# Passing 20 grains of memory from the mixer to the feed-forward, pacing side work behind weight splits, and loading the mixer's weights a unit ahead

## The chip, the cores and the metric

The kernel runs on one core of a Trainium2 chip as a single program. Its engines are TensorE (PE, matrix products), VectorE (DVE), ScalarE (ACT), GpSimd (POOL) and SyncE (SP, which here only issues DMAs). Each works through its own list of instructions strictly in order, waiting where an instruction needs something that another engine or a DMA has not delivered. The metric is the time of one execution on the device in microseconds, smaller being better. Three runs of the kernel before took 2114.45, 2119.53 and 2125.24 us.

## The reference

One transformer-like layer over 2048 tokens of width 1024, all float32:

```python
h = rms_norm(x, norm1); p = h @ w_in                    # 1024 -> 2576
lru_x, lru_g, q, k, v, g, z = split(p)
lru_o = rg_lru(conv4(lru_x), ...) * gelu(lru_g)          # linear recurrence over time
gla_o = rms_norm(gla_chunk_causal(q*s, k, v, log_sigmoid(z @ w_alpha + b)/16)) * silu(g)
x = x + concat([lru_o, gla_o]) @ w_out                   # 1024 -> 1024
h = rms_norm(x, norm2)
gate, up = split(h @ w_ffn_in)                           # 1024 -> 2 x 2816
x = x + (silu(gate) * up) @ w_ffn_out                    # 2816 -> 1024
return rms_norm(x, final_norm)
```

## The kernel before

**Precision.** Every large product is made of three matmuls (`mm3`, L224 to L226). An operand `a` is split into `hi`, a cast to PE's reduced float32R done by ACT (L234), and `lo = a - hi`, done by DVE (L235). PE computes hi*hi, hi*lo and lo*hi. So no matmul of a weight can start before ACT and then DVE have split it, and the split waits for the raw weight's DMA.

**Stages.** The mixer runs over four blocks of 512 tokens (b = 0 to 3, up to about 750 us of the trace). Then the feed-forward's gate and up products run over two blocks of 1024 tokens (about 750 to 1680 us), in a scheme with seven half-size products in place of eight (`Gate.gate_up`), for 22 column groups j each. Then comes the down product (`Down`, to the end), with the same scheme. In a mixer block the feature projections, the gates of the recurrence, the q product, four recurrence scans on DVE (`lru_scan`, L477), the state updates (PE L604, DVE L619), the outputs `lru_out` with their gelus (L634), and the output product of the previous block follow each other. Norm1 of the next block loads x (L240), squares it on ACT (L195, which writes its squares into a scratch piece of memory), takes an rsqrt on DVE and scales x (L279).

**Memory.** Nearly all of the on-chip memory is two regions, cut into grains of 128 words per partition: `A` (tile `arena`, float32, 144 grains: raw loads, activations, scratch) and `R` (tile `arena_r`, float32R, 260 grains: split operands). `Space.alloc` picks free grains when the program is written, and prefers grains that were freed long ago (`since`, with a cost for those freed within the last RECENT = 12 frees). Reusing a grain makes the new writer wait for the last reader of the old contents: an activation, a cast, or a DMA store.

**Weights.** `Feed` keeps two (mixer) or three (gate) split units ready. In the mixer a unit is loaded and split in the same step: `unit` calls `load`, then `split` twice, then frees the raw weight. In the gate stage `gu_makers(j)` fetches four raw pieces and makes seven operands of them (`a11`, `s1`, `s2`, ...; sums at L730, L735, L745, L757), a few units ahead.

**Side work.** Beside the gate products, `spread` deals out other work over the slots (j, r): normalising and transposing the second block's input (`normed`), its differences, and the preparation of the down product's weights (`w2_sums`: sums at L1036, L1040, L1043, a cast on ACT at L1009, a subtraction on DVE at L1016, and two stores to a DRAM tile `w2c` by POOL's queue). `load_acc` loads the down product's accumulators (from `x2d`, by POOL's queue), `split_act` splits its first activations (L1113, L1114).

**Order.** The program is written in Python in one order, and a list scheduler then sets each engine's list by priorities and its own estimates of when things are ready. `tc.issue_after(ins)` makes the scheduler put what is written inside the block behind the instruction `ins`; it adds no wait on the chip. The copies that empty a PSUM bank after a gate product are L907; PE cannot start the next use of that bank earlier.

Of the kernel before, what the change touches and what calls it, by code (L numbers as in the profile page):

```python
# [7 lines left out]
F32 = mybir.dt.float32  # L8
# [29 lines left out]
A_GRAINS = 144  # L38
R_GRAINS = 260
A_BORDER = 48  # L40
# [48 lines left out]
class Space:  # L89
# [6 lines left out]
    def __init__(self, ap, grains):  # L96
        self.ap = ap
        self.n = grains
        self.used = [False] * self.n
        self.since = [0] * self.n  # L100
        self.clock = 0

    def alloc(self, words, key):
        need = -(-words // GRAIN)
        best = None
        run = 0
        for i in range(self.n):
            run = 0 if self.used[i] else run + 1
            if run >= need:
                a = i - need + 1  # L110
                cost = max(0, max(self.since[a : i + 1]) - self.clock + self.RECENT) // self.STEP
                k = (*key(a, need, cost), a)
                if best is None or k < best:
                    best = k
        assert best is not None, f"no room for {words} words; {self.used.count(False) * GRAIN} free"
        a = best[-1]
        for g in range(a, a + need):
            self.used[g] = True
        return self.ap[:, a * GRAIN : a * GRAIN + words], a, need
# [40 lines left out]
def hybrid_layer_kernel(  # L160
# [25 lines left out]

    def bank():
        return pp.tile([P, T], F32, tag="mm", name="mm", bufs=8)
# [42 lines left out]
    def split(src, n, low=False):  # L231
        b = pair(n, low)
        hi, lo = b.r(n)
        nc.scalar.copy(hi, src)  # L234
        nc.vector.tensor_sub(lo, src, hi.bitcast(F32))  # L235
        return b

# [5 lines left out]
    def unit(src, n=D):  # L243
        raw = load(src, n)
# [77 lines left out]

    def block_units(b):
# [17 lines left out]
    feed = Feed([(lambda s=s, n=n: unit(s, n)) for s, n in all_units], 2)  # L341
# [422 lines left out]
    def gu_feed(groups):  # L764
# [12 lines left out]
        def step(i):  # L777
            fetch(i)
            return makers[i]()
# [481 lines left out]
    for b in range(NB):  # L1261
# [7 lines left out]
                  lambda: gate_fetch(0)])  # L1269
    A.aged = True  # L1270
# [3 lines left out]
    for bi, blk in enumerate(blocks):  # L1274
# [14 lines left out]
        else:  # L1289
            spread([w2_sums(range(3, NJ // 2))], [55], 2, NJ - 2)  # L1290
        sums = iter(())
        for js in groups:
# [4 lines left out]
            for r in range(7):  # L1297
                for j, g in zip(js, gens):
                    run(g, 1)
                    for f in side.get((j, r), ()):  # L1300
                        f()
                if js[0] == 0:
                    run(late, 2 if bi else 1)
                if final and nb:
                    run(ahead, 3 if r else 1)
                if final and not nb:
                    if r in (1, 2):
                        down.load_act(r - 1)
                        down.load_acc(r - 1)
                    if r == 3:  # L1310
                        run(down.split_act(0))
# [75 lines left out]
```

## Time and profile before

| what | value |
|---|---|
| runs, median of 3 | 2119.53 us (2114.45 to 2125.24) |
| profiled execution, its own time | 2122.03 us |
| span of that execution, first to last instruction | 2120.3 us |
| PE busy | 2024.7 us (95%) |
| DVE busy | 1343.9 us (63%) |
| ACT busy | 888.5 us (42%) |
| mean granted TensorE clock | 0.981 of 2.4 GHz |

Read it from PE: it is the only engine near its limit, so the time is PE's work, plus the time in which it waited, plus what it lost while its clock stood at half. The average shares of the other engines say little; what matters is which instruction of theirs PE waited for, and what that one had waited for.

### The profile page before, as it was taken

Reading aid. Unit: us, or ns where it says so; the run is one execution under the profiler, and the core shown is the slowest. Engines: PE = TensorE matmul, PEld = TensorE weight load, DVE = VectorE, ACT = ScalarE, POOL = GpSimd, SP = SyncE. Lnnn points to the kernel's source line nnn. Section 1 sums busy time; section 2 is a strip of 40 time slices with the busy share of each in tenths; the row PEclk is TensorE's granted clock in tenths of the full one; section 3 lists DMA queues with packets and bytes.
Section 4 is the critical chain, followed back from the end, with each engine's and each line's share of the span. In section 5 each row is a group of like instructions: output and inputs, shape, how many; then the busy total and the mean of one; then the engine's idle time right before and its main releaser. Section 6 shows DMA issues by size and latency. Waiting matters only on the chain. (4 is left out here: it accounts for less than half of the span.)

```text
span 2120.3 us, 26570 instructions
## 1 busy us (share of the span) xinstructions
PE 2024.7 (95%) x9520; PEld 1661.4 (78%) x9520; DVE 1343.9 (63%) x2390; ACT 888.5 (42%) x1523; POOL 180.0 (8%) x216
## 2 busy tenths in 40 slices
PE   7889999979999999999999999999999999999997
PEld 6778778868887888887787887787778788888876
DVE  6475556555646586557776777677666465665676
ACT  5645635543573453443443554444433221121331
POOL 0000000000000000000111001111110222222110
PEclk9989999989999999999999999999999999999999
DMA  5132245234525553467557457567554946745632
GB/s 181 61 107 82 90 131 178 96 109 134 171 65 169 173 197 107 159 218 219 194 168 229 141 169 240 175 198 224 196 181 143 382 160 219 236 149 172 234 127 80
DMA packets 211174, 353.21 MB, mean 167 GB/s; under 512 B 19409, under 2 KB 95458, under 8 KB 211042
## 3 DMA queue, kind: packets, MB, share of 16 engines
q1 hardware_dynamic: 196898, 304.32, 45.0%
q0 software_dynamic: 14144, 47.20, 5.9%
q8 instruction: 74, 1.21, 0.2%
q14 instruction: 58, 0.48, 0.1%
HBM read 244.49 MB, written 106.95 MB: 166 GB/s over the span
## 5 line engine op out<-in xcount | busy, mean ns | idle before, releaser
L224 PE MATMUL mm<-arena_r 128*128 128x512 f32 (+1 forms) x2848 | 1116.4, 393 | 60.0 <-ACT arena_r L234 33.4
L225 PE MATMUL mm<-arena_r 128*128 128x512 f32 (+1 forms) x2848 | 1108.7, 389 | 6.5 <-DVE arena_r L235 4.8
L226 PE MATMUL mm<-arena_r 128*128 128x512 f32 (+1 forms) x2848 | 1102.6, 389 | 8.4 <-DVE arena_r L235 8.3
L224 PEld LDWEIGHTS mm<-arena_r 128*128 128x128 f32 x2848 | 540.9, 190 | 192.4 <-ACT arena_r L234 37.8
L234 ACT CAST arena_r<-arena 128x512 fp32r<-128x512 f32 (+1 forms) x638 | 377.4, 610 | 647.0 <-PE mm L225 341.4
L226 PEld LDWEIGHTS mm<-arena_r 128*128 128x128 f32 x2848 | 541.1, 190 | 120.5 <-DVE arena_r L235 12.0
L225 PEld LDWEIGHTS mm<-arena_r 128*128 128x128 f32 x2848 | 542.4, 190 | 112.8 <-DVE arena_r L235 9.6
L235 DVE TENSOR_TENSOR arena_r<-arena,arena_r 128x512 fp32r<-128x512 f32 (+1 forms) x638 | 422.1, 677 | 289.2 <-ACT arena_r L234 251.8
L1147 DVE TENSOR_TENSOR arena<-arena,mm 128x512 f32<-128x512 f32 x288 | 197.3, 687 | 149.1 <-PE mm L226 149.1
L1113 ACT CAST arena_r<-arena_r 128x896 fp32r<-128x896 f32 (+1 forms) x88 | 80.2, 916 | 307.5 <-PE mm L225 209.0
L1018 POOL DMA_DIRECT2D w2c<-arena x148 | 79.8, 541 | 870.7 <-ACT arena L1009 792.4
L1114 POOL TENSOR_TENSOR arena_r<-arena_r 128x896 fp32r<-128x896 f32 x40 | 85.6, 2140 | 314.6 <-PE mm L226 123.4
L195 ACT ACTIVATE arena<-arena 128x512 bf16<-128x512 f32 (+1 forms) x80 | 57.0, 712 | 75.0 <-DVE arena L1147 22.7
L907 ACT COPY arena<-mm 128x512 f32<-128x512 f32 x132 | 76.6, 580 | 14.4 <-PE mm L226 14.3
L1009 ACT CAST arena<-arena 128x512 fp32r<-128x512 f32 x74 | 45.6, 620 | 60.0 <-DMA w2c<-arena 13.8
L930 DVE TENSOR_TENSOR arena<-mm,arena 128x512 f32<-128x512 f32 x44 | 30.3, 689 | 56.9 <-PE mm L226 56.9
L626 POOL COPY stc<-arena 128x256 f32<-128x256 f32 x4 | 4.3, 1068 | 644.6 <-DVE arena L619 457.9
L1114 DVE TENSOR_TENSOR arena_r<-arena_r 128x896 fp32r<-128x896 f32 (+1 forms) x48 | 49.0, 1020 | 13.7 <-ACT arena_r L1113 11.4
L1016 DVE TENSOR_TENSOR arena<-arena 128x512 fp32r<-128x512 f32 x74 | 49.8, 688 | 12.2 <-ACT arena L1009 11.6
L730 DVE TENSOR_TENSOR arena<-arena 128x512 f32<-128x512 f32 x44 | 30.2, 687 | 26.3 <-DMA arena<-in_wgu_dram 15.3
L933 DVE TENSOR_TENSOR arena<-mm,arena 128x512 f32<-128x512 f32 x44 | 30.3, 689 | 23.7 <-PE mm L226 23.6
L922 DVE TENSOR_TENSOR arena<-mm,arena 128x512 f32<-128x512 f32 x44 | 30.2, 687 | 23.1 <-PE mm L226 23.1
(132 smaller groups left out, 1067.2 us busy)
## 6 DMA issues: line engine op xcount, KB each, us to landing
arena<-in_wgu_dram SPq DMA_DIRECT2D x176, 256.0 KB, 3.9
ad<-arena SPq DMA_DIRECT2D x148, 256.0 KB, 3.0
w2c<-arena POOLq DMA_DIRECT2D x148, 256.0 KB, 3.8
arena_r<-w2c SPq DMA_DIRECT2D x148, 256.0 KB, 5.3
arena_r<-ad SPq DMA_DIRECT2D x80, 448.0 KB, 3.5
arena<-in_wf_dram SPq DMA_DIRECT2D x40, 512.0 KB, 3.5
arena<-in_wo_dram SPq DMA_DIRECT2D x32, 512.0 KB, 3.9
arena<-in_w_dram SPq DMA_DIRECT2D x44, 256.0 KB, 4.0
```

Of the source, the lines that this page charges most:

```text
L195: nc.scalar.activation(b.ap.bitcast(BF16), src, AF.Square, accum_out=dst)
L224: nc.tensor.matmul(ps, lhsT=sh, rhs=mh, start=first, stop=False, skip_group_check=again)
L225: nc.tensor.matmul(ps, lhsT=sh, rhs=ml, start=False, stop=False, skip_group_check=again)
L226: nc.tensor.matmul(ps, lhsT=sl, rhs=mh, start=False, stop=last, skip_group_check=again)
L234: nc.scalar.copy(hi, src)
L235: nc.vector.tensor_sub(lo, src, hi.bitcast(F32))
L907: nc.scalar.copy(b.f(), ps[:, :n])
L1016: nc.vector.tensor_sub(b.f().bitcast(F32R), b.f(), hi.f())
L1018: nc.gpsimd.dma_start(w2c[k][:, m, i * T : (i + 1) * T], part.f())
L1113: nc.scalar.copy(hi, v)
L1114: (nc.gpsimd if i == 1 else nc.vector).tensor_tensor(lo, v, hi.bitcast(F32), op=ALU.subtract)
L1147: nc.vector.tensor_add(c, c, ps)
```

## The change

20 of the 144 grains of `A` become a separate tile, `swing`. During the mixer it is float32R and belongs to `R` (280 grains, `A` 124); before the gate products it is given back (`shrink`) and allocated anew as float32 in `A` (144 and 260 as before). Grains that were never used now count as freed long ago. The mixer's feed becomes `Units`: the raw weight of the next unit is loaded (`fetch`) before the present one is split, so two raw weights are held. `paced` writes side work behind the instructions of the last gate weight's split (both the ACT cast and the DVE subtraction, kept in `b.ins`), and each gate weight's making behind the split before it. The loads of the first two accumulators move from the last column group to group NJ - 3, and the second block's 55 pieces of weight preparation end one group earlier.

```diff
--- before.py
+++ after.py
@@ -35,8 +35,10 @@
 NCOL = 49
 
 GRAIN = 128
-A_GRAINS = 144
+A_GRAINS = 124
 R_GRAINS = 260
+
+SWING = 20
 A_BORDER = 48
 R_BORDER = 204
 
@@ -94,18 +96,34 @@
     STEP = 3
 
     def __init__(self, ap, grains):
-        self.ap = ap
-        self.n = grains
-        self.used = [False] * self.n
-        self.since = [0] * self.n
+        self.parts = []
+        self.used = []
+        self.since = []
         self.clock = 0
+        self.extend(ap, grains)
+
+    @property
+    def n(self):
+        return len(self.used)
+
+    def extend(self, ap, grains):
+        self.parts.append((self.n, ap))
+        self.used += [False] * grains
+        self.since += [-self.RECENT] * grains
+
+    def shrink(self):
+
+        first, _ = self.parts.pop()
+        assert not any(self.used[first:])
+        del self.used[first:], self.since[first:]
 
     def alloc(self, words, key):
         need = -(-words // GRAIN)
+        starts = {first for first, _ in self.parts}
         best = None
         run = 0
         for i in range(self.n):
-            run = 0 if self.used[i] else run + 1
+            run = 0 if self.used[i] else 1 if i in starts else run + 1
             if run >= need:
                 a = i - need + 1
                 cost = max(0, max(self.since[a : i + 1]) - self.clock + self.RECENT) // self.STEP
@@ -116,7 +134,8 @@
         a = best[-1]
         for g in range(a, a + need):
             self.used[g] = True
-        return self.ap[:, a * GRAIN : a * GRAIN + words], a, need
+        first, ap = max((p for p in self.parts if p[0] <= a), key=lambda p: p[0])
+        return ap[:, (a - first) * GRAIN : (a - first) * GRAIN + words], a, need
 
     def free(self, b):
         self.clock += 1
@@ -184,6 +203,11 @@
     A = Arena(Space(cp.tile([P, A_GRAINS * GRAIN], F32, name="arena"), A_GRAINS), A_BORDER)
     R = Arena(Space(cp.tile([P, R_GRAINS * GRAIN], F32R, name="arena_r"), R_GRAINS), R_BORDER)
 
+    def swing(dtype):
+        return cp.tile([P, SWING * GRAIN], dtype, tag="swing", name="swing", bufs=1)
+
+    R.space.extend(swing(F32R), SWING)
+
     def bank():
         return pp.tile([P, T], F32, tag="mm", name="mm", bufs=8)
 
@@ -231,17 +255,24 @@
     def split(src, n, low=False):
         b = pair(n, low)
         hi, lo = b.r(n)
-        nc.scalar.copy(hi, src)
-        nc.vector.tensor_sub(lo, src, hi.bitcast(F32))
+        b.ins = [nc.scalar.copy(hi, src).ins, nc.vector.tensor_sub(lo, src, hi.bitcast(F32)).ins]
         return b
+
+    pace = []
+
+    def paced(f, *args):
+
+        with ExitStack() as st:
+            for ins in pace:
+                st.enter_context(tc.issue_after(ins))
+            return f(*args)
 
     def load(src, n, low=False, queue=nc.sync):
         b = A.alloc(n, low)
         queue.dma_start(b.f(n), src)
         return b
 
-    def unit(src, n=D):
-        raw = load(src, n)
+    def unit(raw, n):
         v = raw.f(2, n // 2)
         b = [split(v[:, i, :], n // 2) for i in range(2)]
         A.free(raw)
@@ -319,6 +350,25 @@
             b = self.ready.pop(0)
             self.fill()
             return b
+
+    class Units(Feed):
+
+
+        def __init__(self, units, ahead):
+            self.units = list(units)
+            self.raws = []
+            super().__init__([lambda n=n: self.make(n) for _, n in units], ahead)
+
+        def fetch(self):
+            if self.units:
+                self.raws.append(load(*self.units.pop(0)))
+
+        def make(self, n):
+            if not self.raws:
+                self.fetch()
+            raw = self.raws.pop(0)
+            self.fetch()
+            return unit(raw, n)
 
     def block_units(b):
         u = [(wkz[i], 544) for i in range(4)]
@@ -338,7 +388,7 @@
 
     all_units = [u for b in range(NB) for u in block_units(b)]
     all_units += [(wo[n, i], D) for n in range(2) for i in range(4)]
-    feed = Feed([(lambda s=s, n=n: unit(s, n)) for s, n in all_units], 2)
+    feed = Units(all_units, 2)
 
     wal_b, zta_b = A.alloc(256), A.alloc(T)
     nxt = Norm1(0, 2)
@@ -776,7 +826,9 @@
 
         def step(i):
             fetch(i)
-            return makers[i]()
+            b = paced(makers[i])
+            pace[:] = b.ins
+            return b
 
         return Feed([lambda i=i: step(i) for i in range(len(makers))], 3), fetch
 
@@ -1267,6 +1319,8 @@
                   lambda: first.load_x(2)])
     prev.half(1, [lambda: run(first.combine(1)), lambda: first.load_x(3), lambda: run(first.combine(2)),
                   lambda: gate_fetch(0)])
+    R.space.shrink()
+    A.space.extend(swing(F32), SWING)
     A.aged = True
     late = first.combine(3)
     run(late, 1)
@@ -1287,7 +1341,9 @@
             spread([nb.differences(c) for c in range(4)], [6] * 4, 8, 12)
             spread([w2_sums(range(3))], [23], 12, NJ - 2)
         else:
-            spread([w2_sums(range(3, NJ // 2))], [55], 2, NJ - 2)
+            spread([w2_sums(range(3, NJ // 2))], [55], 2, NJ - 3)
+            for i in range(2):
+                side.setdefault((NJ - 3, 3 * i + 1), []).append(lambda i=i: down.load_acc(i))
         sums = iter(())
         for js in groups:
             gens = [blk.gate_up(j) for j in js]
@@ -1298,17 +1354,16 @@
                 for j, g in zip(js, gens):
                     run(g, 1)
                     for f in side.get((j, r), ()):
-                        f()
+                        paced(f)
                 if js[0] == 0:
-                    run(late, 2 if bi else 1)
+                    paced(run, late, 2 if bi else 1)
                 if final and nb:
-                    run(ahead, 3 if r else 1)
+                    paced(run, ahead, 3 if r else 1)
                 if final and not nb:
                     if r in (1, 2):
                         down.load_act(r - 1)
-                        down.load_acc(r - 1)
                     if r == 3:
-                        run(down.split_act(0))
+                        paced(run, down.split_act(0))
                     if r:
                         run(ahead, 2)
                 run(sums, 1)
```

The changed program has as many instructions on each engine as before; what differs is their order and where their data lie. Three places follow. The kernel's lines have moved: L195, L234/L235, L477, L575, L591, L634 of before are L219, L258, L527, L625, L641, L684 after; in the gate stage L730, L745, L757, L922, L927, L1036, L1040, L1043 and L1016 are L780, L795, L807, L974, L979, L1088, L1092, L1095 and L1068.

First, ACT in block 0, from the recurrence's exponentials (L575) to the first gelu (L634). L234 here casts the weights of `lru_out`, L195 squares the next block's x, L591 empties the q product's bank. Before:

```order
L575 ACTIVATE arena<-arena,sc_a 128x512 x4
L195 ACTIVATE arena,ss<-arena 128x1024 x3
L591 ACTIVATE arena<-mm 128x512 x2
L195 ACTIVATE arena,ss<-arena 128x1024
L234 CAST arena_r<-arena 128x512 x8
L634 ACT_TABLE_LOAD
```

After:

```order
L625 ACTIVATE arena<-arena,sc_a 128x512 x4
L629 COPY arena<-mm 128x512
L258 CAST arena_r<-arena 128x512
L258 CAST swing<-arena 128x512
L219 ACTIVATE arena,ss<-arena 128x1024 x4
L641 ACTIVATE arena<-mm 128x512 x2
L258 CAST swing<-arena 128x512 x2
L258 CAST arena_r<-arena 128x512
L684 ACT_TABLE_LOAD
```

Two casts of weights have moved ahead of the four squarings; the next two stand behind them.

Second, SP around the end of block 2's recurrence (in_x_dram: x; in_wf_dram: weights of `lru_out` and of the feature projections; in_wo_dram and in_wg_dram: weights of the output product and of the gate g). Before:

```order
L240 DMA arena<-in_wf_dram 128x1024 x2
L240 DMA arena<-in_x_dram 128x1024 x3
L240 DMA arena<-in_x_dram 128x512
L240 DMA arena<-in_x_dram 128x1024
L240 DMA arena<-in_x_dram 128x512 x2
L240 DMA arena<-in_wo_dram 128x1024 x3
L240 DMA arena<-in_wg_dram 128x1024 x2
```

After:

```order
L272 DMA arena<-in_wv_dram 128x1024
L272 DMA arena<-in_wo_dram 128x1024
L272 DMA arena<-in_wf_dram 128x1024 x2
L272 DMA arena<-in_x_dram 128x1024
L272 DMA arena<-in_x_dram 128x512
L272 DMA arena<-in_x_dram 128x1024 x2
L272 DMA arena<-in_x_dram 128x512 x3
L272 DMA arena<-in_wo_dram 128x1024
L272 DMA arena<-in_wg_dram 128x1024 x3
```

The first output weight has moved ahead of the x loads and of two other weights.

Third, DVE in the gate stage, at the product of the fourth kind for one column group (L922 adds it up; L235 subtracts for a weight split; L1036 and L1043 belong to `w2_sums`, L730, L735 and L745 to the gate weights' sums). Before:

```order
L235 TENSOR_TENSOR arena_r<-arena,arena_r 128x512
L730 TENSOR_TENSOR arena<-arena 128x512
L735 TENSOR_TENSOR arena<-arena 128x512
L1036 TENSOR_TENSOR arena<-arena 128x512
L922 TENSOR_TENSOR arena<-mm,arena 128x512
L235 TENSOR_TENSOR arena_r<-arena,arena_r 128x512
L1043 TENSOR_TENSOR arena<-arena 128x512
L745 TENSOR_TENSOR arena<-arena 128x512
L235 TENSOR_TENSOR arena_r<-arena,arena_r 128x512
L927 TENSOR_TENSOR arena<-mm,arena 128x512
```

After:

```order
L258 TENSOR_TENSOR arena_r<-arena,arena_r 128x512
L1088 TENSOR_TENSOR arena<-arena 128x512
L807 TENSOR_TENSOR swing<-arena,swing 128x512
L258 TENSOR_TENSOR arena_r<-swing,arena_r 128x512
L974 TENSOR_TENSOR arena<-mm,arena 128x512
L258 TENSOR_TENSOR arena_r<-arena,arena_r 128x512
L1092 TENSOR_TENSOR arena<-arena 128x512
L1068 TENSOR_TENSOR arena<-arena 128x512
L780 TENSOR_TENSOR swing<-arena 128x512
L979 TENSOR_TENSOR arena<-mm,arena 128x512
```

The preparation's first sum (L1036, now L1088) no longer stands directly ahead of L922: the split of one more gate weight (L258) lies between them, and the weights' own sum L730 (now L780) belongs to a later unit.

## Rows read from the trace of the kernel before

**Rows 1.** The page, part 1: busy time, share and instructions of each engine.

```profile
PE 2024.7 (95%) x9520; PEld 1661.4 (78%) x9520; DVE 1343.9 (63%) x2390; ACT 888.5 (42%) x1523; POOL 180.0 (8%) x216
```

**Rows 2.** What PE waited for: us in total, times, longest.

```profile
PE mm L224 <- ACT arena_r L234: 33.4, 9, 13.7
PE mm L224 <- ACT arena L907: 9.6, 7, 3.4
PE mm L226 <- DVE arena_r L235: 8.3, 6, 3.0
```

**Rows 3.** PE's timeline, blocks 0 to 2: start, length, [idle before, releaser].

```profile
111.74 0.80 PE L224 MATMUL mm<-arena_r 128*128 128x512 f32 x1 [12.74 <-ACT arena_r L234]
114.21 0.80 PE L226 MATMUL mm<-arena_r 128*128 128x512 f32 x1 [1.26 <-DVE arena_r L235]
...
251.91 0.80 PE L225 MATMUL mm<-arena_r 128*128 128x512 f32 x1 [4.13 <-DVE arena_r L235]
...
254.93 0.40 PE L224 MATMUL mm<-arena_r 128*128 128x512 f32 x1
255.16 0.40 PE L225 MATMUL mm<-arena_r 128*128 128x512 f32 x1
...
453.87 0.80 PE L224 MATMUL mm<-arena_r 128*128 128x512 f32 x1 [13.67 <-ACT arena_r L234]
...
458.60 0.63 PE L225 MATMUL mm<-arena_r 128*128 128x512 f32 x1
```

**Rows 4.** SP's queue, blocks 0 and 2: first issue, stretch of the group.

```profile
88.33 14.72 SPq L240 DMA_DIRECT2D arena<-in_x_dram  x3
103.16 11.96 SPq L240 DMA_DIRECT2D arena<-in_wf_dram  x4
...
447.51 7.99 SPq L240 DMA_DIRECT2D arena<-in_wo_dram  x3
```

**Rows 5.** DVE's timeline, blocks 0 and 2.

```profile
100.33 2.33 DVE L477 TENSOR_TENSOR_SCAN arena<-arena 128x512 f32<-128x512 f32 x2
...
441.66 2.45 DVE L477 TENSOR_TENSOR_SCAN arena<-arena,carry 128x512 f32<-128x512 f32 x2
```

**Rows 6.** ACT's timeline, the mixer's blocks.

```profile
106.47 1.06 ACT L195 ACTIVATE arena<-arena 128x1024 bf16<-128x1024 f32 x1 [1.68 <-DMA arena<-in_x_dram]
...
453.19 1.14 ACT L234 CAST arena_r<-arena 128x512 fp32r<-128x512 f32 x2 [4.43 <-DMA arena<-in_wo_dram]
...
548.47 0.74 ACT L234 CAST arena_r<-arena 128x272 fp32r<-128x272 f32 x2 [3.47 <-DMA arena<-in_wkz_dram]
```

**Rows 7.** Stretches: us, busy (x) of PE, PEld, DVE, ACT, POOL; PEclk, DMA, GB/s.

```profile
250.00:300.00 50.00, 44.25 (x231) 33.92 (x232) 29.31 (x76) 17.20 (x34) 1.31 (x1) 0.97 0.44 147
550.00:600.00 50.00, 47.71 (x275) 41.60 (x274) 32.62 (x64) 32.72 (x56) 0.00 (x0) 0.97 0.56 185
640.00:690.00 50.00, 46.12 (x251) 37.38 (x244) 32.91 (x70) 15.95 (x30) 0.40 (x1) 0.93 0.52 176
750.00:1600.00 850.00, 828.72 (x3606) 672.95 (x3606) 594.71 (x947) 369.30 (x644) 79.26 (x147) 0.99 0.59 187
1250.00:1300.00 50.00, 46.97 (x196) 38.30 (x195) 33.76 (x54) 19.89 (x36) 7.04 (x14) 0.93 0.56 175
```

**Rows 8.** ACT and DVE in the gate stage and at the down product's start.

```profile
1122.82 0.62 ACT L1009 CAST arena<-arena 128x512 fp32r<-128x512 f32 x1 [4.16 <-DMA w2c<-arena]
...
1281.07 0.69 DVE L1036 TENSOR_TENSOR arena<-arena 128x512 f32<-128x512 f32 x1 [2.41 <-DMA arena<-in_w_dram]
...
1525.47 0.69 DVE L730 TENSOR_TENSOR arena<-arena 128x512 f32<-128x512 f32 x1 [3.41 <-DMA arena<-in_wgu_dram]
...
1681.11 1.09 DVE L1114 TENSOR_TENSOR arena_r<-arena_r 128x896 fp32r<-128x896 f32 x1 [4.84 <-ACT arena_r L1113]
```

**Rows 9.** The page, part 5: busy, mean ns | idle before, releaser.

```profile
L234 ACT CAST arena_r<-arena 128x512 fp32r<-128x512 f32 (+1 forms) x638 | 377.4, 610 | 647.0 <-PE mm L225 341.4
...
L907 ACT COPY arena<-mm 128x512 f32<-128x512 f32 x132 | 76.6, 580 | 14.4 <-PE mm L226 14.3
```

## The prediction

> **What bounds the kernel now.** I read the busy times first. PE is busy for 95% of the span, DVE for 63%, ACT for 42% [rows 1], so only PE's list can set the end, and there is 2120.3 - 2024.7 = 95.6 us in which it does nothing. Then I read what PE waited for [rows 2]: over a third of that, 33.4 us in nine waits, is for ACT's casts of operands (L234), 8.3 us for DVE's half of the same split, 9.6 us for the copies that empty a bank (L907). PE seldom waits because ACT or DVE is too slow. It waits because the instruction it needs stands in their lists behind one that waits for a DMA.
>
> Third, the clock. After a long wait the matmuls start at half rate, 1.2 instead of 2.4 GHz: after block 1's wait of 4.13 us, seven matmuls take from 251.91 to 254.93, 3.02 us, where at the full rate, one every 0.23 us as from 254.93 on, they would take 1.6 [rows 3]. So a wait of 4.1 us costs 5.6. After block 2's 13.67 us ten matmuls take 4.73 us instead of 2.3 up to 458.60, so it costs at least 16.1.
>
> **The change part by part.**
>
> *Block 0, 99 to 114 us.* PE has nothing from 99.00 to 111.74 but for a weight of `lru_out`, and 1.26 us more for the next [rows 3]. SP shows why: the weight's load is issued at 103.16, behind three x loads drawn out over 14.72 us [rows 4], because the x loads wait for memory that the scans free, and the scans end at 102.66 [rows 5]. ACT squares the last x at 106.47 [rows 6] before it casts. After the change the weights are loaded a unit earlier, and two casts stand ahead of the squarings. DVE's subtractions still stand behind the scans. So PE gets its first operand at 102.66, plus 0.13 for the carry's copy and 0.69 for the subtraction, about 103.5: a wait of 4.5 us where there were 14.0. With the clock, by the two events above: 14.0 + 2.5 = 16.5 before, 4.5 + 1.4 = 5.9 after. Gain 10.6. What follows is covered: two casts are ready, one half of two units each, and the third unit's load needs only the first subtraction. That load gets until 103.5 plus 48 matmuls (10.9 us at full rate), and the four loads there took 11.96 us together, 3.0 each [rows 4].
>
> *Block 2, 440 to 454 us.* The same picture with the output weights: the load is issued at 447.51, behind the x loads of the order above and a squaring whose scratch memory it reuses, and the cast at 453.19 has waited 4.43 us for it [rows 4, 6]. After, that load stands ahead of the x loads and the cast ahead of the squarings. The scans, ending at 441.66 + 2.45 = 444.11 [rows 5], are next: PE, free at 453.87 - 13.67 = 440.20, waits until about 444.8. 4.6 + 1.4 = 6.0 instead of 16.1: gain 10.1.
>
> *Blocks 1 and 3.* PE's wait of 4.13 us ends with a subtraction that stands behind the scans, before and after: nothing gained. The stretch 640 to 690 (3.88 us idle, clock 0.93) is bound by the same and stays [rows 7]. What goes in block 1 is a chain behind it: each output weight's raw piece reused one region, so its load waited for the split before. 50 - 44.25 - 4.13 = 1.6 us of idle in 250 to 300 [rows 7] and what the chain costs after 300; two alternating regions break it. Taken 3, bounds 0 and 5.
>
> *The gelus.* In 550 to 600 PE idles 2.3 us and loses 3% of its clock, 1.5 us [rows 7]: a cast at 548.47 waited 3.47 us for a load [rows 6] with a gelu behind it, whose bank PE needs. Loaded a unit ahead the cast does not wait. Gain 3, bounds 0 and 4. The casts of the feed-forward's input ahead of the last gelu near 740 are the same case; another 3, bounds 0 and 4.
>
> *The gate stage.* 750 to 1600 holds 850 - 828.72 = 21.3 us of idle, and a clock of 0.99, some 8 us: 3.5 of it in 1250 to 1300 alone, at 0.93 [rows 7]. About 29 in all. Three waits show three causes [rows 8]. A cast of weight preparation (L1009) waits 4.16 us because it writes memory that a store to `w2c` still reads; the weight cast and the bank copy stand behind it. A preparation sum (L1036) waits 2.41 us for a load ahead of L922 and a split. A sum for the weights themselves (L730) waits 3.41 us for its load. The change works on all three: with 20 more grains than the mixer leaves, all counted as old, stores and raw weights get more time. Counted in instructions, a gate weight's load stands at least 8 splits ahead of its use but for one case (12 stood at one), a region of L1009 is reused at least 4 stores after its last (ten were at one or two), and side work is written behind a split rather than ahead of it. I leave 5 us for what is late next, mostly DVE's subtraction just before PE's use: gain 24, bounds 0 and 29.
>
> *Nothing for the rest.* `shrink` makes the first write of the float32 tile wait for the last product that reads the float32R one, 12 matmuls before the mixer's end; two a11 products of 12 matmuls, 2.7 us each, cover the some 2 us of sum, cast and subtraction. If they don't, it is one wait of 2 us. The accumulators move little on POOL's queue. At the down product's start L1114 waits until 1681.11 for a cast that waits for its load [rows 8], with L1147 behind it; it stands there in both orders. Bounds -3 and +4.
>
> Sum: 10.6 + 10.1 + 3 + 3 + 3 + 24 = 53.7. From the profiled execution's 2122.0 (1.7 us around its span) this gives 2068.3. That execution is 2.5 us above the median of the three runs, so I forecast **2066 us**. The bounds of the terms reach from 2066 - 12 = 2054 to 2066 + 39 = 2105 if all fell on one side.
>
> **The rivals.**
>
> *The gate stage keeps its waits (A).* Side work pushed behind splits also frees memory later, and the wait for a store or a load only changes places. For it: ACT's casts idle 341.4 us for PE to free operands in `R` [rows 9], so a split is often late by itself, and all behind it with it. Against it: ACT is busy 369.3 of 850 us there [rows 7]. The term of 24 is gone: 2090.
>
> *The mixer keeps its waits (B).* `A` has 20 grains fewer there and holds two raw weights instead of one. A load whose memory is not free stands at the head of SP's list and holds up the rest, as the three x loads did for 14.72 us [rows 4]. Terms of 29.7 gone: 2096. The Trainium skill ("DMA: Bandwidth & Descriptors", section on the anatomy of one DMA) has the rule that speaks against the change here: a semaphore wait is done by the issuing sequencer before dispatch, and the DMA engines merely consume what they are given. By it, issuing earlier gains nothing when the memory is not free earlier; it only moves the blockage ahead of more loads. The trace agrees (the weight's load at 103.16 follows the last x load at once), and by the rule alone the sum would be this rival's.
>
> *Both (C).* Within 10 us of before, 2115.
>
> *Slower (D).* Side work behind a split lands right ahead of the bank copies L907, of which there are 132 [rows 9]. PE now waits for seven of them, 9.6 us [rows 2]. If each copy came one cast of 0.61 us [rows 9] after PE needs the bank, 132 x 0.61 = 80 us would be added to the 2066: 2146. It decides from 0.5 us a copy on, where 66 us make up for all gains and 0.5% more. Against it: ACT's load, and the second bank that PE has meanwhile.
>
> **How the numbers follow.** Forecast 0.55, A 0.15, B 0.13, C 0.09, D 0.08. About 0.5% (10.6 us) is what a measurement can tell from no change. Forecast, A and B are all under 2109: faster 0.83; C is same, 0.09; D slower, 0.08. The range goes up to 2098, so that A and B lie within and C and D, 0.17, without. It goes down to 2045: the 2054 of all good bounds, less 9 if the subtractions of blocks 1 and 3 also come out ahead of the scans (5.6 and part of 3.88). Within the forecast's own case I expect 2052 to 2080.
>
> **What would show it.** Right: PE's two long waits near 100 and 440 us become 4 to 5 us each, ending with a subtraction (L235's successor) just behind the scans; PE's total for casts falls from 33.4 to about 10; the stage 750 to 1600, ending some 50 us earlier, idles under 6 us with a clock of 1.00; L1009's successor no longer waits for a store. Wrong: a new wait on SP in the mixer with x loads or weights drawn out over more than 10 us; copies L907's successor with more than 9.6 us of PE's waits; a busy PE that loses its time to the clock alone.

## The result, and the profile after

The changed kernel takes 2056.15 us (median of four runs, 2054.72 to 2061.93), the kernel before 2119.61 us in the same comparison. The ratio is 0.9705 with an interval of 0.9674 to 0.9736, so it is some 63 us faster. The forecast was 2066.

First the busy times of the changed kernel, in the page's part 1, to be laid beside [rows 1]:

```profile
span 2055.1 us, 26677 instructions
PE 2004.1 (98%) x9520; PEld 1652.2 (80%) x9520; DVE 1335.3 (65%) x2390; ACT 884.0 (43%) x1523; POOL 178.0 (9%) x216
```

The span is 65.2 us shorter. PE's idle time falls from 95.6 to 2055.1 - 2004.1 = 51.0 us, 44.6 less. The other 20.6 us come out of its busy time, with the same matmuls. Some 12 of them are the clock: by the clock records of the two traces PE was busy at half rate for 47.2 us before and for 23.6 us after, and half of the difference is what that cost; the mean clock rises from 0.981 to 0.991. The rest is not shown. A part goes with the number of PE's waits, 53 before and 25 after, since a matmul right behind a wait counts as busy for 0.50 or 0.80 us in the rows below, where 0.40 is usual.

What PE waited for after the change; [rows 2] answer to it (L248 to L250 are the three matmuls, L258 the split, L529 the copy beside the scans, L1199 the down product's sums, L959 the bank copies):

```profile
PE mm L249 <- DVE carry L529: 8.0, 2, 4.1
PE mm L248 <- DVE arena L1199: 8.0, 6, 4.3
PE mm L249 <- DVE arena_r L258: 5.6, 2, 4.2
PE mm L248 <- ACT arena L959: 0.9, 1, 0.9
```

The 33.4 us for casts are gone from the list, the copies cost 0.9 in place of 9.6. The longest wait, 9.8 us for the first x at the kernel's start, is in both kernels. What else is left of size are three waits of some 4 us at the scans, and the down product's start. "carry L529" and "L258" are one thing here: a subtraction for a weight and the tiny copy before it, both right behind the scans (but for one wait of 1.4 us at 755 us). A stretch over the gate stage, beside [rows 7]:

```profile
700.00:1560.00 860.00, 857.65 (x3792) 701.67 (x3791) 619.45 (x995) 390.05 (x685) 82.71 (x153) 1.00 0.61 197
```

2.35 us of idle in 860 where there were 21.3 in 850, and the full clock.

PE's timeline at the ends of the recurrences of blocks 0, 1 and 2, beside [rows 3]:

```profile
101.81 0.50 PE L248 MATMUL mm<-arena_r 128*128 128x512 f32 x1
...
106.24 0.51 PE L250 MATMUL mm<-arena_r 128*128 128x512 f32 x1 [0.92 <-DVE arena_r L258]
...
242.59 0.80 PE L249 MATMUL mm<-arena_r,swing 128*128 128x512 f32 x1 [4.20 <-DVE arena_r L258]
...
428.49 0.50 PE L249 MATMUL mm<-arena_r 128*128 128x512 f32 x1 [4.14 <-DVE carry L529]
```

And what DVE did just before the first and the third of these waits ended, beside [rows 5]:

```profile
103.21 2.33 DVE L527 TENSOR_TENSOR_SCAN arena<-arena 128x512 f32<-128x512 f32 x2
...
425.34 2.46 DVE L527 TENSOR_TENSOR_SCAN arena<-arena,carry 128x512 f32<-128x512 f32 x2
427.71 0.13 DVE L529 COPY carry<-arena 128x1 f32<-128x1 f32 x1
427.76 0.68 DVE L258 TENSOR_TENSOR arena_r<-arena,arena_r 128x512 fp32r<-128x512 f32 x1
```

The 13.67 us of block 2 have become the 4.14 us of block 1: PE resumes as soon as the subtraction behind the scans is through.

### The profile page after: what moved, and what is told of

Its sections match the earlier page's. It is cut to its first block, busy times and chain, and to the rows that moved or that the text cites. A ratio compares the mean times of both kernels' runs of the same rounds, so it can differ in the third digit from the quotient of the medians.

```text
span 2055.1 us, 26677 instructions
## 1 busy us (share of the span) xinstructions
PE 2004.1 (98%) x9520; PEld 1652.2 (80%) x9520; DVE 1335.3 (65%) x2390; ACT 884.0 (43%) x1523; POOL 178.0 (9%) x216
## 4 chain that ended last, share of the span: by engine, by line
PE 89%; DVE 4%; ACT 2%; DMA 2%; issue 1%; POOL 0%; DVEq 0%; SPq 0%; POOLq 0%; ACTq 0%
PE mm L248 29%; PE mm L249 29%; PE mm L250 29%; DMA arena_r<-w2c 1%; DVE arena L527 1%; PE mm L858 1%; DMA arena_r<-ad 1%; DVE arena L525 0%; DVE arena L526 0%; PE mm L329 0%; ACT arena L622 0%; PE mm L600 0%; PE mm L710 0%; PE mm L576 0%; DVE arena_r L258 0%
## 5 line engine op out<-in xcount | busy, mean ns | idle before, releaser
L249 PE MATMUL mm<-arena_r 128*128 128x512 f32 (+1 forms) x2596 | 1004.6, 387 | 9.4 <-DVE carry L529 8.0
L250 PE MATMUL mm<-arena_r 128*128 128x512 f32 (+1 forms) x2584 | 998.3, 388 | 0.9 <-DVE arena_r L258 0.9
L248 PE MATMUL mm<-arena_r 128*128 128x512 f32 (+1 forms) x2512 | 980.2, 391 | 9.0 <-DVE arena L1199 8.0
L249 PEld LDWEIGHTS mm<-arena_r 128*128 128x128 f32 x2596 | 489.9, 189 | 104.7 <-DVE carry L529 8.9
L248 PEld LDWEIGHTS mm<-arena_r 128*128 128x128 f32 x2512 | 473.3, 189 | 121.8 <-DVE arena L1199 13.6
L250 PEld LDWEIGHTS mm<-arena_r 128*128 128x128 f32 x2584 | 487.9, 189 | 100.7 <-DVE arena_r L258 1.3
L258 ACT CAST arena_r<-arena 128x512 fp32r<-128x512 f32 (+1 forms) x465 | 277.3, 612 | 461.5 <-PE mm L249 241.2
L258 DVE TENSOR_TENSOR arena_r<-arena,arena_r 128x512 fp32r<-128x512 f32 (+1 forms) x464 | 308.9, 677 | 217.8 <-ACT arena_r L258 204.1
L1199 DVE TENSOR_TENSOR arena<-arena,mm 128x512 f32<-128x512 f32 x272 | 186.3, 686 | 142.6 <-PE mm L250 142.5
L258 ACT CAST arena_r<-swing 128x512 fp32r<-128x512 f32 x90 | 55.8, 621 | 106.8 <-PE mm L249 37.3
L219 ACT ACTIVATE arena<-arena 128x512 bf16<-128x512 f32 (+1 forms) x64 | 46.9, 733 | 81.8 <-DVE arena L1199 26.0
L258 ACT CAST swing<-arena 128x512 fp32r<-128x512 f32 (+1 forms) x83 | 48.1, 593 | 70.2 <-PE mm L250 30.3
L258 DVE TENSOR_TENSOR arena_r<-swing,arena_r 128x512 fp32r<-128x512 f32 x90 | 61.7, 687 | 22.9 <-ACT arena_r L258 18.7
L249 PE MATMUL mm<-arena_r,swing 128*128 128x512 f32 x164 | 65.3, 398 | 4.2 <-DVE arena_r L258 4.2
L959 ACT COPY arena<-mm 128x512 f32<-128x512 f32 x100 | 58.4, 584 | 22.8 <-PE mm L250 21.9
L248 PE MATMUL mm<-swing,arena_r 128*128 128x512 f32 (+1 forms) x164 | 60.5, 369 | 3.8 <-DVE arena_r L284 2.2
L248 PE MATMUL mm<-arena_r,swing 128*128 128x512 f32 x156 | 62.5, 402 | 0.0
L982 DVE TENSOR_TENSOR arena<-mm,arena 128x512 f32<-128x512 f32 x43 | 29.7, 691 | 50.3 <-PE mm L250 50.3
L250 PE MATMUL mm<-swing,arena_r 128*128 128x512 f32 (+1 forms) x168 | 61.2, 365 | 0.0
```

The lines of the kernel that those rows point to most:

```text
L219: nc.scalar.activation(b.ap.bitcast(BF16), src, AF.Square, accum_out=dst)
L248: nc.tensor.matmul(ps, lhsT=sh, rhs=mh, start=first, stop=False, skip_group_check=again)
L249: nc.tensor.matmul(ps, lhsT=sh, rhs=ml, start=False, stop=False, skip_group_check=again)
L250: nc.tensor.matmul(ps, lhsT=sl, rhs=mh, start=False, stop=last, skip_group_check=again)
L258: b.ins = [nc.scalar.copy(hi, src).ins, nc.vector.tensor_sub(lo, src, hi.bitcast(F32)).ins]
L959: nc.scalar.copy(b.f(), ps[:, :n])
```

## The experiments

Twelve runs. Five take a part out of the change, three put one part alone into the kernel before (the exchange of grains comes with the ages there), one puts the two large parts into it, and three follow what the profile after suggests. The "before" of each ratio ran on the same chip.

| kernel | us, median | ratio to before, interval |
|---|---|---|
| changed | 2056.15 | 0.9705 (0.9674 to 0.9736) |
| changed, no pacing | 2086.97 | 0.9842 (0.9813 to 0.9871) |
| changed, no early loads | 2075.71 | 0.9789 (0.9768 to 0.9810) |
| changed, ages from 0 | 2061.88 | 0.9721 (0.9700 to 0.9742) |
| changed, no exchange of grains | 2059.06 | 0.9710 (0.9693 to 0.9727) |
| changed, accumulators as before | 2054.93 | 0.9703 (0.9684 to 0.9721) |
| before + exchange and ages | 2096.84 | 0.9907 (0.9879 to 0.9935) |
| before + early loads | 2086.55 | 0.9859 (0.9831 to 0.9886) |
| before + pacing | 2086.14 | 0.9857 (0.9825 to 0.9888) |
| before + early loads + pacing | 2057.94 | 0.9713 (0.9692 to 0.9734) |
| changed + later scans | 2046.89 | 0.9674 (0.9645 to 0.9704) |
| the same again | 2052.74 | 0.9672 (0.9654 to 0.9690) |
| changed + later scans + later split | 2050.90 | 0.9686 (0.9663 to 0.9709) |

**Pacing taken out.**

```diff
         with ExitStack() as st:
-            for ins in pace:
-                st.enter_context(tc.issue_after(ins))
+            pass
             return f(*args)
```

> The changed kernel without its pacing: side work and the making of gate weights are written with nothing that holds them behind a split; all else as changed. Theory (pacing): the gate stage's gain of some 30 us comes from holding side work behind splits, so most of it is lost, PE waits again some 15 to 20 us in that stage with a clock under 1, and the time is about 2056 + 20 = 2076 us. Rival (memory): the waits went because stores and raw weights get older memory, from the 20 grains and their ages; then pacing is worth under 5 us and the time stays at 2056 to 2061 us. The mixer is the same by both.

31 us slower, more than expected. Its gate stage idles again, 850 - 823.51 = 26.5 us:

```profile
740.00:1590.00 850.00, 823.51 (x3586) 668.10 (x3586) 592.87 (x943) 366.13 (x636) 82.25 (x152) 0.99 0.58 188
```

ACT's timeline in it shows the old cause (L1060 is the preparation's cast, L258 the weight's, L958 the bank's copy), beside [rows 8]:

```profile
1093.27 0.62 ACT L1060 CAST arena<-arena 128x512 fp32r<-128x512 f32 x1 [3.78 <-DMA w2c<-arena]
1093.80 0.61 ACT L258 CAST arena_r<-swing 128x512 fp32r<-128x512 f32 x1
1094.32 0.58 ACT L958 COPY arena<-mm 128x512 f32<-128x512 f32 x1
```

So older memory did not remove these waits; the theory of pacing holds.

**Pacing alone, in the kernel before** (`paced` and `b.ins` as in the change, nothing else).

> The kernel before with side work and gate weights paced, and nothing else; the mixer is as before. Theory (pacing alone clears the gate stage): 2119 - 25 to 30, 2089 to 2094 us, with the idle time of 750 to 1600 us under 8 us. Rival (pacing needs the older memory): without the 20 old grains the casts still wait for stores, and the time is 2100 to 2115 us.

32 us faster; the rival falls. Its stage has no idle time to speak of, with the old 144 and 260 grains:

```profile
750.00:1600.00 850.00, 849.67 (x3749) 694.73 (x3748) 607.09 (x975) 377.78 (x664) 82.26 (x152) 1.00 0.60 191
```

The groups of instructions show what has changed. The preparation's cast (L1019 here, L1009 of before) and the weights' sum (L738 here) wait for nothing at all, columns as in [rows 9]:

```profile
L1019 ACT CAST arena<-arena 128x512 fp32r<-128x512 f32 x74 | 45.7, 618 | 0.0
L738 DVE TENSOR_TENSOR arena<-arena 128x512 f32<-128x512 f32 x44 | 30.1, 685 | 0.0
```

In the kernel with early loads alone the same cast still waits 60.7 us in all:

```profile
L1027 ACT CAST arena<-arena 128x512 fp32r<-128x512 f32 x74 | 45.3, 621 | 60.7 <-DMA w2c<-arena 11.4 <-DMA arena<-in_w_dram 10.2 <-DVE arena L1054 9.9
```

My reading of these rows: when such an instruction comes to the head of its list, its load or store is done, because the weight split ahead of it has waited longer than the DMA takes. ACT's idle time has not gone. In 750 to 1550 us, before and then with pacing alone:

```profile
L234 ACT CAST arena_r<-arena 128x512 fp32r<-128x512 f32 x320 | 194.9, 621 | 333.8 <-PE mm L225 265.1 <-issue 25.9 <-PE mm L226 16.3
L1009 ACT CAST arena<-arena 128x512 fp32r<-128x512 f32 x68 | 41.8, 620 | 52.7 <-DVE arena_r L235 11.4 <-DVE arena L1036 9.2 <-DMA ad<-arena 9.2
```
```profile
L234 ACT CAST arena_r<-arena 128x512 fp32r<-128x512 f32 x328 | 198.8, 621 | 386.3 <-PE mm L225 205.6 <-issue 65.0 <-DVE arena L753 23.4
```

The preparation's casts have lost 52.7 us of it, and the weights' casts have 52.5 more, where PE waits for almost none of it. But the part that ends with PE has fallen from 265.1 to 205.6 us. That it is the wait for PE which covers the DMAs is therefore argued and not shown.

**Early loads taken out.**

```diff
             raw = self.raws.pop(0)
-            self.fetch()
             return unit(raw, n)
```

> The changed kernel with each mixer weight loaded in the step that splits it, as before the change; the 20 grains and the pacing stay. Theory (loads): the mixer's gain of some 35 us is the earlier load, so the long waits near 100 and 440 us and the chain of block 1 come back for the most part, and the time is about 2056 + 25 to 35, 2081 to 2091 us. Rival (memory): with 20 grains more for split operands and old grains preferred the loads find room early enough by themselves, and the time is 2056 to 2066 us.

20 us slower, less than the theory's 25 to 35 and far more than the rival's. And the theory fails in the place it named: the long waits do not come back. What comes back are short waits of PE at several units, up to 2.3 us for a cast and 1.1 us for a subtraction, for loads just too late, as in block 2's features (PE, then the cast before it):

```profile
395.93 0.49 PE L248 MATMUL mm<-arena_r 128*128 128x512 f32 x1 [1.15 <-ACT arena_r L258]
```
```profile
391.08 0.62 ACT L258 CAST swing<-arena 128x512 fp32r<-128x512 f32 x1 [4.06 <-DMA arena<-in_wv_dram]
```

PE's idle time in all is 2074.0 - 2015.8 = 58.2 us, only 7.2 more than in the changed kernel; the other 11.7 us of the longer span are in its busy time.

**The exchange alone, and the early loads alone, in the kernel before** (`Space`, `swing`, `shrink` as in the change, which bring the ages with them; then `Units` as in the change).

> The kernel before with the exchange of 20 grains and the ages alone; weights loaded as before, no pacing. The run without early loads kept only short waits near 100 and 440 us, so early loads alone cannot be what removed the 13 us waits. Theory (either suffices): the room of 280 grains for split operands lets the weights be split ahead of the scans too; the long waits near 99 and 440 us fall to about 4 us each, the rest stays, and the time is about 2119 - 20 to 25, 2094 to 2099 us. Rival (early loads needed): without early loads the long waits stay and the time is 2110 to 2120 us.

> The kernel before with the mixer's weights loaded a unit ahead, and nothing else. Theory (either suffices): the two long waits fall to 4 to 5 us each and the chain of block 1 goes, the gate stage keeps its 30 us; the time is 2119 - 30 to 35, 2084 to 2089 us. Rival (room needed too): two raw weights in flight and 260 grains for split operands block each other, one of the long waits stays, and the time is 2095 to 2110 us.

2096.84 and 2086.55 us, both times as the theory had them. Block 2's long wait with the exchange alone:

```profile
438.55 0.50 PE L248 MATMUL mm<-arena_r 128*128 128x512 f32 x1 [4.14 <-DVE carry L502]
```

The time of the exchange alone came out right partly by luck. "The rest stays" was not so: from the same matmul to the same matmul of PE, the mixer is only 11.8 us shorter in its trace, about 740 us it gains 3.9 more, and 8.9 us come from the gate stage, which has less idle time without any pacing:

```profile
735.00:1585.00 850.00, 832.41 (x3646) 675.25 (x3645) 606.63 (x964) 377.29 (x658) 80.94 (x150) 1.00 0.60 191
```

The same grains and ages without pacing in the changed kernel lengthen that stage by 4.3 us against before, and early loads alone shorten it by 5.7. So the stage moves by several us with each of these new orders of the lists, and a share of the exchange in it is not shown.

So the two long waits have two sufficient cures: the exchange with its ages, which lets the weight be split before the squarings, or an earlier load. With pacing alone both are still there, 12.84 and 13.85 us:

```profile
111.68 0.80 PE L224 MATMUL mm<-arena_r 128*128 128x512 f32 x1 [12.84 <-ACT arena_r L234]
...
455.03 0.80 PE L224 MATMUL mm<-arena_r 128*128 128x512 f32 x1 [13.85 <-ACT arena_r L234]
```

**Early loads and pacing together.**

> The kernel before with the early loads and the pacing together; without the 20 grains, the ages and the moved accumulator loads. Theory (two parts, each in its own stage): the gains add, about 31 + 32 us, so 2118 - 63 = 2055 us, within 4 us of the whole change. Rival (the exchange gives pacing its room): without it some gate waits stay, and the time is 2062 to 2075 us.

2057.94 us. The two parts add within the spread of the runs: 31 + 32 us alone, 58 together by the medians; 30 + 30 and 61 by the ratios. One wait is longer than in the changed kernel, in block 0 (block 2's 4.14 us are two waits here, 2.86 and 0.75):

```profile
106.19 0.79 PE L226 MATMUL mm<-arena_r 128*128 128x512 f32 x1 [3.90 <-DVE carry L505]
```

**No exchange; ages from 0; accumulators back.** Three small parts out of the change: `A_GRAINS = 144` without `swing`; `self.since += [0] * grains`; `load_acc` beside `load_act` again and the spread to `NJ - 2`.

> The changed kernel without the exchange of grains: 144 grains float32 and 260 float32R throughout, as before; loads a unit ahead and pacing stay. Theory (loads): the 20 grains matter little, the time is 2053 to 2061 us. Rival (room): without them the weights split early find no free operand memory in the mixer, casts wait for PE to free operands, and the waits near 100 and 440 us come back in part: 2066 to 2081 us.

> The changed kernel with unused grains counted as freed just now (0) and not as old. Theory (pacing and loads): the ages decide only the first use of a grain, so the time is 2053 to 2060 us. Rival (memory): the 20 grains that come into the float32 region before the gate products carry an age of 0 as before, the clock of frees is far beyond it by then, and only the start of the kernel differs; what could be lost is in the first 100 us, up to 10 us, 2056 to 2066 us.

> The changed kernel with the first two accumulators loaded, and the weight preparation ended, where the kernel before has them. Theory: nothing, 2053 to 2060 us; the wait at the down product's start stays about 4 us either way, since it is for activations. Rival: the accumulators' loads collide there with the weights' loads and the wait grows by 3 to 6 us, 2060 to 2066 us.

2059.06, 2061.88 and 2054.93 us. All three intervals overlap that of the changed kernel, so none of these is shown to move the time. With ages from 0 the time lies outside the theory's range and in the rival's, and its trace has a wait of 4.18 us at 118 us, for the next block's scaled x, where the changed kernel waits for at most 0.45 at a time. A cost of the ages of some 6 us by the medians stays open. Without the exchange block 0 has the 4 us wait just shown; that is all it can be seen to buy here.

**Scans later.** PE's remaining waits of 4 us end with a subtraction behind the scans. So I moved the scans:

```diff
-        hs = [lru_scan(b, f, gts[f]) for f in range(4)]
+        hs = [lru_scan(b, f, gts[f]) for f in range(4 if b == 0 else 2)]
         ...
             qs.append(q)
+        if b > 0:
+            hs += [lru_scan(b, f, gts[f]) for f in (2, 3)]
+            if b + 1 < NB:
+                after = Norm1(b + 1)
```

> The changed kernel with one edit of mine: in blocks 1 to 3 the last two recurrence scans and the next block's Norm1 are written behind the q product, so that the subtractions of the output weights stand between the two pairs of scans on DVE. Theory (PE's waits of 4.1 us in blocks 1, 2 and 3 are for subtractions behind the scans): the three waits and the half rate after them go, 3 x 5.6 = 17 us; with something lost to a later Norm1 the time is 2040 to 2048 us. Rival (the wait is for what the scans free, or what is late next takes their place): the waits move to the casts or to the x loads and the time is 2052 to 2062 us.

> The kernel with the later scans once more, with more rounds, since its interval met that of the changed kernel. Theory (two of the three waits behind the scans are gone): a ratio of 0.965 to 0.968 against before and an interval that ends below 0.9705, the changed kernel's ratio; 2042 to 2048 us. Rival (the first measurement was low by its spread): 0.969 to 0.971, 2051 to 2056 us.

2046.89 and then 2052.74 us, ratios 0.9674 and 0.9672. This beats the kernel before. Against the changed one the ratios are about 0.3% lower, 6 to 7 us, but the intervals (up to 0.9690 here, from 0.9674 there) overlap, so a gain over it is not shown. The second run's ratio is as its theory had it, its time is not: 2052.74 us lies in the rival's range, with a kernel before of 2121.08 us beside it. What is shown is where the waits went. DVE in block 1 of the first run shows the subtractions between the two pairs of scans, and PE has no wait there any more:

```profile
236.31 0.13 DVE L529 COPY carry<-arena 128x1 f32<-128x1 f32 x1
236.36 0.68 DVE L258 TENSOR_TENSOR arena_r<-arena,arena_r 128x512 fp32r<-128x512 f32 x1
...
237.62 0.68 DVE L258 TENSOR_TENSOR arena_r<-arena,arena_r 128x512 fp32r<-128x512 f32 x1
238.22 1.28 DVE L525 SCALAR_TENSOR_TENSOR arena<-arena 128x512 f32<-128x512 f32 x2
```

The waits of blocks 1 and 2 are gone in both runs' traces, that of block 3 is not (3.41 and 4.17 us). There the q product's copy stands behind casts that wait for their loads (PE, then ACT):

```profile
605.16 0.50 PE L248 MATMUL mm<-arena_r 128*128 128x512 f32 x1 [3.41 <-ACT arena L641]
```
```profile
603.48 1.14 ACT L258 CAST swing<-arena 128x512 fp32r<-128x512 f32 x2 [1.26 <-DMA arena<-in_wo_dram]
604.52 0.59 ACT L641 ACTIVATE arena<-mm 128x512 f32<-128x512 f32 x1
```

**Split later at the down product's start**, on top of the later scans.

```diff
-                nc.vector.tensor_add(c, c, ps)
+                self.added = nc.vector.tensor_add(c, c, ps).ins
         ...
-                    if r in (1, 3, 5):
+                    if at == 0 and r in (3, 5):
+                        with tc.issue_after(self.added):
+                            run(nxt, 1)
+                    elif at and r in (1, 3, 5):
                         run(nxt, 1)
```

> The kernel with the later scans, and a second edit of mine: at the first step of the down product the split of the next activations is put behind the fourth accumulation on DVE, where it stood behind the second. Theory (the accumulation L1199 of the changed kernel waits only because a split that waits for its load stands ahead of it): the wait of 4 us and the half rate behind it go, 5 to 7 us, 2040 to 2042 us. Rival (the split itself is then late for its own products, or the load is what bounds): the wait comes back one step later, 2045 to 2048 us.

2050.90 us, no gain, and outside both ranges. The wait has grown to 5.18 us, and a split that waits for its load still stands ahead of the accumulations (DVE, then ACT):

```profile
1604.88 1.09 DVE L1170 TENSOR_TENSOR arena_r<-arena_r 128x896 fp32r<-128x896 f32 x1 [5.59 <-ACT arena_r L1169]
1605.89 1.88 DVE L1203 TENSOR_TENSOR arena<-arena,mm 128x512 f32<-128x512 f32 x3
1607.68 2.38 DVE L1170 TENSOR_TENSOR arena_r<-arena_r 128x896 fp32r<-128x896 f32 x1
```
```profile
1603.91 0.94 ACT L1169 CAST arena_r<-arena_r 128x896 fp32r<-128x896 f32 x1 [5.64 <-DMA arena_r<-ad]
```

The edit held the wrong split. It moved that of the second step's activations behind the fourth accumulation, where it now runs at 1607.68 us. The one that PE's wait goes back to belongs to the third step: its load is issued at 1598.17 us, behind those of the first two steps. With the later scans alone the same instruction stands behind the second accumulation:

```profile
1601.95 1.28 DVE L1170 TENSOR_TENSOR arena_r<-arena_r 128x896 fp32r<-128x896 f32 x1 [4.33 <-ACT arena_r L1169]
```

So neither the theory nor the rival was tested on it. What the rival named shows in one new wait only, 0.98 us at 1615.81 us, for the second half of the split that was moved.

## Why the prediction was right

Sign and places held, the causes in part; the sum of 53.7 was 10 us short. The two traces can be laid side by side, PE's n-th matmul before against its n-th after, since its order differs in 426 places of 9520 only and the same matmuls stand ahead of each point used here. Gains below "by the trace" are such differences, each from one execution. By the prediction's own steps:

- *Gate stage.* Forecast 24 of the 29 us there; by the trace 30.3, and 32.7 with pacing alone, whose median is 32 us below before. This is the term that was most too small. I left 5 us for what would be late next, and 2.35 us of idle is what is left. And 29 was itself too low a bound: the idle 21.3 us and the half rate, 15.8 us that cost 7.9, make 29.2, and what lies beyond that these rows do not price. Of the three means that the step named, holding work behind splits is sufficient alone and needed; of grains and ages no share is shown.
- *Block 2.* Forecast a wait of 4.6 us behind the scans, measured 4.14, ending as described. Gain by the trace 10.5, forecast 10.1.
- *Block 0.* Forecast 4.5 us and the half rate behind it, measured 0.92 and no half rate. This step's wait was too long by 3.6 us, and with the half rate the step was off by about 5 us: by the trace 16.0 are gained there and 2.9 lost right behind, forecast 10.6. I counted PE's next operand as split behind the scans. PE had one split already, and worked on it from 101.81 until 106.24 - 0.92 = 105.32; the scans even ended later than before, at 103.21 + 2.33 = 105.54 instead of 102.66. Without the exchange the wait is 3.90 us, near the 4.5 that I had reckoned, and the gain by the trace 10.7.
- *Cause of the two long waits.* The step said early loads. They suffice, but so does the exchange with its ages, which the prediction gave no share in the mixer.
- *Block 1's chain.* Forecast 3, bounds 0 and 5; by the trace 6.7, and 7.2 with early loads alone. The term was too small.
- *The gelus.* Forecast 3 and 3; by the trace 3.4 near 550 us and 3.9 near 740. The second came true by another cause than the one named: early loads alone gain nothing there, because the cast ahead of that gelu waits for the feed-forward's input, which is no mixer weight, and pacing alone gains 3.7. Near 550 us pacing alone gains 2.5 as well, so the share of the early loads there stays open. PE near 740 us before and with early loads alone, then the cast in the latter:

```profile
742.42 0.50 PE L224 MATMUL mm<-arena_r 128*128 128x512 f32 x1 [1.98 <-ACT arena L634]
```
```profile
713.17 0.64 PE L224 MATMUL mm<-arena_r 128*128 128x512 f32 x1 [2.19 <-ACT arena L652]
```
```profile
712.00 0.62 ACT L234 CAST arena_r<-arena 128x512 fp32r<-128x512 f32 x1 [3.99 <-DMA arena<-xq0b]
```

- *Blocks 1 and 3.* Forecast unchanged: 4.20 us after, 4.13 before in block 1.
- *Down product's start, accumulators.* Forecast nothing, within -3 to +4. The wait is 4.3 us where it was 3.9, and the accumulators' place makes no difference.
- *Not foreseen.* At the very start PE has a wait of 2.24 us; by the trace 2.8 us are lost there. Early loads alone have the same wait, the exchange alone has none. On DVE a weight's subtraction now stands right ahead of the instruction that PE needs first (L284):

```profile
18.25 0.59 PE L248 MATMUL mm<-swing,arena_r 128*128 128x272 f32 x1 [2.24 <-DVE arena_r L284]
```

Rival B, that SP's waiting for memory would merely hold up more loads, did not come about. In block 0 SP's last two x loads still wait for the scans, but the weights are in front of them, beside [rows 4]:

```profile
100.94 3.91 SPq L272 DMA_DIRECT2D arena<-in_x_dram  x2
```

What decided was which load stands in front, not how many wait. The rule of the Trainium skill ("DMA: Bandwidth & Descriptors", the anatomy of one DMA), that the issuing sequencer waits for semaphores before it dispatches, agrees with this row.

## What to carry to other kernels

When an engine at 95% waits, look at what stands in front of the instruction it waited for: in the rows here it was a needed cast, copy or sum behind an instruction that waited for a DMA. Work that is not urgent is best put behind an instruction that has to wait for the bottleneck anyway; here its own DMAs were done by the time it ran. Before giving two parts of a change their shares, run each alone: two here cured the same wait, and two others, taken out, changed nothing that could be measured. And look at where a part's time went as well as at its median: the exchange alone met its forecast with a third of its gain from a stage that it was not meant for. Before an edit that moves an instruction, make sure that it is the one that the wait goes back to.

## What the runs showed of the hardware

Waits of nearly one length cost PE different amounts of clock. The 4.13 us of block 1 before were followed by 3.0 us at half rate. After the change the 4.20 us of block 1 were followed by more than 5, all these rows being 0.43 us apart, where the full rate is 0.23:

```profile
243.19 0.63 PE L250 MATMUL mm<-arena_r 128*128 128x512 f32 x1
243.61 0.63 PE L249 MATMUL mm<-arena_r,swing 128*128 128x512 f32 x1
...
247.45 0.63 PE L249 MATMUL mm<-arena_r,swing 128*128 128x512 f32 x1
247.88 0.63 PE L250 MATMUL mm<-swing 128*128 128x512 f32 x1
```

And after the 4.14 us of block 2 PE ran at the full rate for a microsecond before it fell, and was back at 432.93:

```profile
429.07 0.39 PE L249 MATMUL mm<-arena_r 128*128 128x512 f32 x1
429.30 0.42 PE L250 MATMUL mm<-arena_r 128*128 128x512 f32 x1
...
429.94 0.63 PE L249 MATMUL mm<-arena_r 128*128 128x512 f32 x1
430.37 0.63 PE L250 MATMUL mm<-arena_r 128*128 128x512 f32 x1
...
432.93 0.41 PE L250 MATMUL mm<-arena_r 128*128 128x512 f32 x1
```

So the 1.4 us that the prediction put down for the half rate after a 4 us wait is one draw of several: against 0.23 us a matmul these two lost 2.9 and 1.7 us. Over the whole kernel the half rate gave back some 12 us (half of 47.2 - 23.6) beside 44.6 us of waits, about one for four.
